# Output weight's sums on VectorE, three row groups prepared a quarter ahead, VectorE's order pinned in the output stage, results left in loaded operands

## The chip, the cores and the metric

The kernel runs on one core of a Trainium2 chip. A core has TensorE (PE, matrix products into PSUM banks), VectorE (DVE), ScalarE (ACT), GpSimd (POOL) and SyncE (SP), whose queue issues most of the DMAs. The metric is the device time of one execution in microseconds; lower is better.

## The reference

One layer of a decoder block on x of 2048 tokens by 1024 channels, in float32:

```python
mod = jax.nn.silu(c) @ w_ada + b_ada
shift, scale, gate = jnp.split(mod, 3, axis=-1)
h = rms_norm(x, norm_w) * (1.0 + scale) + shift
z = h @ w_in
a, b, g_conv, q, k, v, g_attn, m_conv, m_attn = jnp.split(z, SPLIT_POINTS, axis=-1)
u = depthwise_causal_conv(a * jax.nn.sigmoid(b), conv_w, conv_b)     # 31 taps
u = jax.nn.silu(layer_norm(u, conv_ln_w, conv_ln_b)) * jax.nn.silu(g_conv)
y_conv = u @ w_conv_out
# three groups of four heads, dilated causal windows, merged by their softmax denominators
o = ...
y_attn = (o * jax.nn.silu(g_attn)) @ w_attn_out
y = jax.nn.sigmoid(m_conv) * y_conv + jax.nn.sigmoid(m_attn) * y_attn
out = y @ w_out
x = x + gate * out
```

Only the last three products matter here: u @ w_conv_out, the merge into y, and y @ w_out with the gate and the residual.

## The kernel before

**Precision.** A float32 matrix product is made of three float32r products: each operand is split into a high part (ScalarE copies it into float32r, "h") and a low part (a subtraction, "l"), and h·h, h·l and l·h are added up in PSUM.

**The quarters.** The convolution branch is projected for four quarters of 512 tokens (`t` = 0 to 3), each in eight blocks `dm` of 128 output channels. A block is 24 matmuls of 512 columns (`project`, L1231) into a bank `yc`; six banks take turns. Behind a block VectorE multiplies the bank by the loaded gate `mc` (L1482), adds the loaded attention half `yl` (L1483), and SP stores the result to `y_d` (L1484). `yl` and the result `yc` both take their buffers from a ring of four named `yt`; `mc` has a ring of three.

**Normalising a quarter ahead.** While a quarter is projected, class `Norm` prepares the next: mean and squares on VectorE (`d`, `red`), a matmul `pc` of the squares, a copy `stf` on VectorE (L1269), two steps on GpSimd (L113, L114), a matmul `pr` that spreads the factor over the columns (L1276), and then per channel group `vf`, `tv` and the parts `u_kh`, `u_kl`. `d` is in the pool `lnp`, two buffers.

**The output stage.** y @ w_out is computed by a seven-product scheme on quarters of both matrices. For eight `j` (`out_quad`), token blocks j and j + 8 form four quarters of y, which are loaded as `yq`, combined on GpSimd (`ys`, L1422 to L1427) and split into `yh`, `yl` (`y_split`, L1431 and L1432). The weight's seven combinations are called B11, B21, T1, T2, T3, B22 and T4; each is held as `woh`/`wol` (or `wohi`/`wolo`) tiles for four row groups k. Products run in the order 0, 3, 2, 1, 4, 5, 6 on three banks: oa takes products 0, 2, 4 and 6, oc takes 3 and 5, ob takes 1. The sums of a bank go on growing from product to product, and between them VectorE adds the bank to a tile `xt`, which was loaded with the residual x (L1491); `xt` then goes to the output (L1496). So product 2, 4 and 6 each wait until VectorE has added what stood in oa.

**Preparing the weight.** `wo_fetch` loads 1 MB of `w_out` for a row group k (`wo_raw`), `wo_scale` multiplies it by the gate (L1375, two operations of 1024 columns), `wo_first` makes B11, B21 and T1 and computes T1 to T4 in place by four subtractions on GpSimd (L1400), and `wo_rest` splits T2, T3, B22 and T4 (L1390 and L1391). Row group 0 is loaded and scaled in the third quarter; groups 1 to 3 in the last. B22 and T4 can be split only when TensorE has read the last of the tiles whose place they take: in the last block, and at the end of it. The same holds for the parts of y with i from 2 on, which take the places of `u`. A hook `out_hooks(j)(i)` runs inside `product`: the part of y that is five products ahead, in the first quad also B22 (k = 1 and 3 on GpSimd) and T4, and the loads of the next quad.

**What sets the order.** TensorE's instructions stand in the order of the program. On the other engines a scheduler puts them into an order by its own estimate of when each is ready; an instruction passed to `keep_in_program_order` stays behind the one that the program has in front of it on its engine. Each engine then runs its list strictly in order. Pools hand out ring buffers; a DMA into a buffer waits until its last reader is done. `at_block(n, m, f)` calls f at matmul m of block n.

Of the kernel before, what the change touches and what calls it, by code (L numbers as in the profile page):

```python
# [10 lines left out]
F32 = mybir.dt.float32  # L11
F32R = mybir.dt.float32r
# [3 lines left out]
ALU = mybir.AluOpType  # L16
# [38 lines left out]
def tile_hybrid_block(  # L55
# [1244 lines left out]
    def at_block(n, m, f):  # L1300
        plan.setdefault(n, {}).setdefault(m, []).append(f)
# [63 lines left out]
            nc.sync.dma_start(last["gate"][c], gate_d[:, 512 * c : 512 * c + 512].to_broadcast([P, 512]))  # L1365

    def wo_fetch(k):
        w = sp.tile([P, S], F32, tag="wide", name="wo_raw0") if k == 0 else op.tile([P, S], F32, tag="raw", name=f"wo_raw{k}", bufs=4)
        w = wo_raw[k] = w.rearrange("p (h c n) -> p h c n", h=2, c=2)
        nc.sync.dma_start(w, w_out.rearrange("(h k p) (c n) -> k p h c n", h=2, p=P, c=2)[k])  # L1370

# [3 lines left out]
            nc.vector.tensor_tensor(w[:, :, c], w[:, :, c], last["gate"][c][:, None, :].to_broadcast([P, 2, 512]), op=ALU.mult)  # L1375

    def wo_place(name):
        if name in ("B11", "B21"):
            return [wop.tile([P, 4, 512], F32R, name=f"wo{hl}{name}") for hl in "hl"]
        if name == "T1":  # L1380
            return [op.tile([P, 4, 512], F32R, name=f"wo{hl}{name}", bufs=1) for hl in "hl"]
        if name == "T3":
            return [[wcp.tile([P, 512], F32R, tag=f"w{hl}{k}", name=f"wo{hl}{name}{k}") for k in range(4)] for hl in "hl"]
        return [quarter_tile(*{"T2": (0, 2), "B22": (0, 0), "T4": (1, 0)}[name], hl, f"wo{hl}{name}") for hl in ("hi", "lo")]

    def wo_split(name, k, src, eng=nc.vector):
        if name not in wo:
            wo[name] = wo_place(name)
        h, l = (x[k] if isinstance(x, list) else x[:, k] for x in wo[name])
        nc.scalar.activation(h, src, AF.Copy)  # L1390
        eng.tensor_tensor(l, src, h.bitcast(F32), op=ALU.subtract)  # L1391

    def wo_first(k):
        w = wo_raw[k]
        wo_split("B11", k, w[:, 0, 0])
        wo_split("B21", k, w[:, 1, 0])
        t1 = ys.tile([P, 512], F32, tag="fraw", name=f"wot1_{k}", bufs=3)
        for dst, x0, x1 in ((t1, w[:, 0, 1], w[:, 0, 0]), (w[:, 0, 0], w[:, 1, 1], w[:, 0, 1]), (w[:, 0, 1], w[:, 1, 1], t1),
                            (w[:, 1, 0], w[:, 1, 0], w[:, 0, 1])):
            nc.gpsimd.tensor_tensor(dst, x0, x1, op=ALU.subtract)  # L1400
        wo_split("T1", k, t1)

    def wo_rest(name, k, eng=nc.vector):
# [3 lines left out]
    LEAD = 5  # L1407

    def y_load(j):
        t = ysrc[j] = op.tile([P, S], F32, tag="raw", name=f"yq{j}", bufs=4).rearrange("p (q k t) -> p q k t", q=4, t=P)  # L1410
        for b in range(2):
            jj = j + NB // 2 * b
            nc.sync.dma_start(t[:, 2 * b : 2 * b + 2].rearrange("p q k t -> p (q k) t"),
                              y_d[:, :, P * jj : P * jj + P].rearrange("k p t -> p k t"))

    def y_split(j, i):
        a11, a12, a21, a22 = (ysrc[j][:, q].rearrange("p k t -> p (k t)") for q in range(4))
        pool_tt = nc.gpsimd.tensor_tensor
        n = WO_ORDER[i]
        if n == 0:  # L1420
            s1 = ysrc[j, "S1"] = ys.tile([P, 512], F32, tag="fraw", name=f"ys1_{j}", bufs=3)
            pool_tt(s1, a21, a22, op=ALU.add)  # L1422
            pool_tt(a21, a11, a21, op=ALU.subtract)
        if n == 2:
            pool_tt(a11, ysrc[j, "S1"], a11, op=ALU.subtract)
        if n == 4:
            pool_tt(a12, a12, a11, op=ALU.subtract)  # L1427
        src = (a11, a12, a11, ysrc[j, "S1"], a21, a12, a22)[n]
        own, tag, bufs = (op, "y", 2) if (j, i) in ((0, 0), (0, 1)) else (up[1], "u", KC)
        h, l = ya_of[j, n] = [own.tile([P, 512], F32R, tag=tag + hl, name=f"y{hl}{j}_{n}", bufs=bufs) for hl in "hl"]  # L1430
        nc.scalar.activation(h, src, AF.Copy)  # L1431
        nc.vector.tensor_tensor(l, src, h.bitcast(F32), op=ALU.subtract)  # L1432

    ysrc, ya_of, xin = {}, {}, {}

# [9 lines left out]
        xin[j, q] = t  # L1445

    at_block(12, 6, gate_rows)
    at_block(16, 6, lambda: wo_fetch(0))
    at_block(22, 6, lambda: wo_scale(0))

    for t in range(NT):
        tsl = slice(512 * t, 512 * t + 512)
        if t == NT - 1:
            lnp_c.__exit__(None, None, None)
            wop_c, wop = right("wop")
            ap_c.__exit__(None, None, None)
            up_c[1].__exit__(None, None, None)
            op_c = pool("op", bufs=2)
            op = op_c.__enter__()
            for k in range(1, 4):  # L1460
                at_block(KC * t, 2, lambda k=k: wo_fetch(k))
                at_block(KC * t + (1, 2, 3)[k - 1], 1, lambda k=k: wo_scale(k))
            for k in range(4):
                at_block(KC * t + (0, 1, 2, 4)[k], (3, 6, 15, 3)[k], lambda k=k: wo_first(k))
            for i, (name, k) in enumerate((b, k) for b in ("T2", "T3") for k in range(4)):
                at_block(KC * t + 4 + i // 2, 4 + 11 * (i % 2), lambda name=name, k=k: wo_rest(name, k))
            at_block(KC * t + 4, 8, lambda: y_load(0))
            for i in range(2):
                at_block(KC * t + 6, 6 + 6 * i, lambda i=i: y_split(0, i))
            for q in (0, 3):  # L1470
                at_block(KC * t + 5, 8, lambda q=q: x_load(0, q))
        for dm in range(KC):
            gt = gp.tile([P, 512], F32, tag="gt", name=f"mc{t}_{dm}")
            nc.sync.dma_start(gt, mc_d[dm, :, tsl])
            ya = ys.tile([P, 512], F32, tag="yt", name=f"yl{t}_{dm}", bufs=4)
            nc.sync.dma_start(ya, ya_d[dm, :, tsl])
            pz = bank("zso"[dm % 3], f"yc{t}_{dm}")
            sl = slice(P * (dm % 4), P * (dm % 4) + P)
            project(pz, [h[:, sl] for h, _ in wc[dm // 4]], [l[:, sl] for _, l in wc[dm // 4]],
                    norms[t].uh, norms[t].ul, plan.get(KC * t + dm))  # L1480
            yt = ys.tile([P, 512], F32, tag="yt", name=f"yc{t}_{dm}", bufs=4)
            nc.vector.scalar_tensor_tensor(yt, gt, 1.0, pz, op0=ALU.add, op1=ALU.mult)  # L1482
            nc.vector.tensor_add(yt, yt, ya)  # L1483
            nc.sync.dma_start(y_d[dm, :, tsl], yt)  # L1484

    HB = NB // 2

    def out_quad(j, hooks):
        pa, pb, pc = bank("z", f"oa{j}"), bank("s", f"ob{j}"), bank("o", f"oc{j}")
        x11, x12, x21, x22 = (xin.pop((j, q)) for q in range(4))  # L1490
        add = lambda dst, ps: nc.vector.tensor_tensor(dst, dst, ps, op=ALU.add)  # L1491
        begun = set()

        def store(q, t):
            jj, c = j + HB * (q // 2), q % 2
            nc.sync.dma_start(out2[P * jj : P * jj + P, 512 * c : 512 * c + 512], t)  # L1496

        def product(n, ps, more=False):
            yh, yl = ya_of.pop((j, n))
            wh, wl = ([x[k] if isinstance(x, list) else x[:, k] for k in range(4)] for x in wo[PRODUCTS[n][1]])  # L1500
            yh, yl = ([y[:, P * k : P * k + P] for k in range(4)] for y in (yh, yl))
            terms = [t for k in range(4) for t in ((yh[k], wh[k]), (yh[k], wl[k]), (yl[k], wh[k]))]
            for m, (y, w) in enumerate(terms):
                nc.tensor.matmul(ps, y, w, start=(m == 0 and ps.name not in begun), stop=(m == 11 and not more),  # L1504
                                 skip_group_check=True)
            begun.add(ps.name)
            hooks(WO_ORDER.index(n))

        product(0, pa, True)
        add(x11, pa)  # L1510
        product(3, pc, True)
        add(x22, pc)
        product(2, pa, True)
        add(x12, pa)
        product(1, pb)
        add(x11, pb)
        store(0, x11)
        product(4, pa, True)
        add(x22, pa)
        store(3, x22)  # L1520
        product(5, pc)
        add(x12, pc)
        store(1, x12)
        product(6, pa)
        add(x21, pa)
        store(2, x21)

    for q in (1, 2):
        x_load(0, q)
# [3 lines left out]
    def out_hooks(j):  # L1533
        def f(i):
            if j == 0 and i < 2:
                for k in (2 * i, 2 * i + 1):
                    wo_rest("B22", k, (nc.vector, nc.gpsimd)[k % 2])
            elif j == 0 and i < 6:
                wo_rest("T4", i - 2)
            if j + 1 < HB and i == 0:  # L1540
# [15 lines left out]
    wop_c.__exit__(None, None, None)  # L1556
    wcp_c.__exit__(None, None, None)
    hpool_c[0].__exit__(None, None, None)

# [27 lines left out]
```

## Time and profile before

| | |
|---|---|
| time, median of 3 runs | 2428.23 us (2424.98 to 2432.36) |
| profiled execution | 2423.63 us, span 2421.7 us |
| PE / DVE / ACT / POOL busy | 2372.0 / 1734.9 / 998.0 / 839.7 us |
| mean granted TensorE clock | 0.994 |
| last quarter of the projection | about 2205 to 2250 us |
| output stage | about 2250 us to the end |

Times in a timeline are microseconds from the start of the span: start, length, engine, line, operation, written tile <- read tiles, and in brackets how long the engine had been idle and what ended that. Tiles appear there without their numbers, so `yl` is both the loaded attention half and a low part of y; the line tells which.

### The profile page before, as it was taken

To read this page: it belongs to the slowest core of one execution; us is meant where nothing else is said; L and a number is where in the kernel's file an instruction comes from. 1 tells how busy PE (TensorE), PEld (TensorE's weight loads), DVE (VectorE), ACT (ScalarE), POOL (GpSimd) and SP (SyncE) were. 2 spreads that over 40 slices of the span, in tenths; PEclk is the share of its full clock that TensorE was granted. 3 is DMA by queue.
4 is the path that set the end of the run, shared out by engine and by line. 5 is a ranking of instruction groups with operands and counts; after the bars stand their busy time and mean duration, and the time that the engine had idled before them with its cause. 6 is when DMAs were issued, how large, how long until landed. Compare 5 with 4: busy or idle time off the path is not lost. (4 is left out here: it accounts for less than half of the span.)

```text
span 2421.7 us, 39474 instructions
## 1 busy us (share of the span) xinstructions
PE 2372.0 (98%) x12785; PEld 2117.9 (87%) x12785; DVE 1734.9 (72%) x3941; ACT 998.0 (41%) x2790; POOL 839.7 (35%) x949
## 2 busy tenths in 40 slices
PE   6999999999999999999999999999999999999899
PEld 2989999999999999999888888878888888888687
DVE  5865655555555565567779999989999977787643
ACT  4833433343343444344544444554444444431221
POOL 3421111111111111112467777775565620004420
PEclk8999999999999999999999999999999999999999
DMA  7633543454453222115664544674444469865742
GB/s 256 219 115 110 158 128 102 142 150 140 145 154 89 70 67 61 31 49 176 211 207 138 164 154 133 211 231 125 136 150 132 156 221 315 285 198 185 215 145 83
DMA packets 349468, 372.99 MB, mean 154 GB/s; under 512 B 29704, under 2 KB 251176, under 8 KB 349262
## 3 DMA queue, kind: packets, MB, share of 16 engines
q1 hardware_dynamic: 335966, 346.80, 46.1%
q10 hardware_dynamic: 13296, 23.66, 2.7%
q8 instruction: 102, 1.67, 0.3%
q14 instruction: 104, 0.85, 0.1%
HBM read 231.74 MB, written 138.61 MB: 153 GB/s over the span
## 5 line engine op out<-in xcount | busy, mean ns | idle before, releaser
L370 PE MATMUL pz<-wh_u,hT_lo 128*128 128x384 f32 x1536 | 537.1, 350 | 5.2 <-DVE hT_lo L289 3.8
L370 PE MATMUL pz<-wh_u,hT_hi 128*128 128x384 f32 x1536 | 518.3, 337 | 5.3 <-ACT wh_u L346 2.9
L370 PE MATMUL pz<-wl_u,hT_hi 128*128 128x384 f32 x1536 | 518.9, 338 | 0.6 <-DVE wl_u L349 0.6
L398 DVE SCALAR_TENSOR_TENSOR qk<-pz,st,wqk 128x128 f32<-128x128 f32 x384 | 117.0, 346 | 318.3 <-POOL st L114 318.1
L113 POOL TENSOR_SCALAR st<-st 128x2 f32<-128x2 f32 x192 | 47.3, 247 | 812.7 <-ACT sq L387 812.7
L370 PEld LDWEIGHTS pz<-wh_u,hT_hi 128*128 128x128 f32 x1536 | 290.7, 189 | 8.2 <-ACT wh_u L346 3.6
L370 PEld LDWEIGHTS pz<-wh_u,hT_lo 128*128 128x128 f32 x1536 | 289.4, 188 | 8.1 <-DVE hT_lo L289 4.6
L370 PEld LDWEIGHTS pz<-wl_u,hT_hi 128*128 128x128 f32 x1536 | 289.8, 189 | 2.0 <-DVE wl_u L349 1.5
L434 ACT ACTIVATE qkT<-ptq 128x256 f32<-128x256 f32 x192 | 73.6, 383 | 420.2 <-PE ptq L432 419.7
L1033 DVE SCALAR_TENSOR_TENSOR ce<-us,pair_taps,ce 128x512 f32<-128x512 f32 x240 | 179.8, 749 | 1.7
L1004 DVE SCALAR_TENSOR_TENSOR ce<-ut,chan,ce 128x512 f32<-128x512 f32 x240 | 179.5, 748 | 0.0
L1017 DVE SCALAR_TENSOR_TENSOR cq<-ut,chan,cq 128x512 f32<-128x512 f32 x208 | 156.5, 752 | 4.2
L919 POOL TENSOR_TENSOR slT<-wT,shT 128x512 fp32r<-128x512 f32 x97 | 129.4, 1336 | 75.3 <-ACT shT L918 75.3
L387 ACT ACTIVATE sq<-pz 128x128 bf16<-128x128 f32 x384 | 106.0, 276 | 99.6 <-PE pz L370 92.6
L114 POOL TENSOR_TENSOR st<-st,mhalf 128x2 f32<-128x2 f32 x192 | 136.6, 712 | 16.0
L918 ACT ACTIVATE shB<-wB 128x512 fp32r<-128x512 f32 x120 | 75.5, 631 | 152.0 <-issue 44.5
L918 ACT ACTIVATE shT<-wT 128x512 fp32r<-128x512 f32 x100 | 63.1, 631 | 153.0 <-issue 66.2
L919 POOL TENSOR_TENSOR slB<-wB,shB 128x512 fp32r<-128x512 f32 x77 | 102.4, 1330 | 68.5 <-ACT shB L918 67.1
L447 ACT ACTIVATE sm<-sm,osb 128x128 f32<-128x128 f32 (+1 forms) x192 | 88.7, 462 | 62.6 <-DVE osb L445 59.6
L461 PE MATMUL po<-lv,pT 128*128 128x128 f32 x600 | 97.2, 273 | 0.0
L461 PEld LDWEIGHTS po<-lv,pT 128*128 128x128 f32 x600 | 93.0, 189 | 0.5 <-issue 0.5
L445 DVE CUSTOM_DVE_ANT_0 sm<-ps,mask 128x128 f32<-128x128 f32 (+1 forms) x192 | 68.7, 358 | 26.5 <-PE ps L442 26.4
(666 smaller groups left out, 6331.5 us busy)
## 6 DMA issues: line engine op xcount, KB each, us to landing
wB<-in_w_in_dram SPq DMA_DIRECT2D x140, 256.0 KB, 3.3
qkv_d<-qkv SPq DMA_DIRECT2D x128, 192.0 KB, 2.2
wT<-tT_d SPq DMA_DIRECT2D x80, 256.0 KB, 2.7
raw_u<-in_w_in_dram SPq DMA_DIRECT2D x93, 192.0 KB, 2.8
lqk<-qkv_d SPq DMA_DIRECT2D x128, 128.0 KB, 2.3
tT_d<-wB ACTq DMA_DIRECT2D x60, 256.0 KB, 2.8
acc_d<-osb SPq DMA_DIRECT2D x192, 65.0 KB, 1.8
at<-acc_d SPq DMA_DIRECT2D x64, 195.0 KB, 3.5
```

The lines of the kernel that those rows point to most:

```text
L114: nc.gpsimd.tensor_tensor(dst, scratch[:, :n], mhalf[:, :n], op=ALU.pow)
L370: nc.tensor.matmul(pz[:, :width], part(a, k, P * j, P), w[:, :width], start=(m == 0), stop=(m == 23))
L387: nc.scalar.activation(sq, pz[:, P * i : P * i + P], AF.Square, scale=1.0 / math.sqrt(P), accum_out=st[:, i : i + 1])
L398: nc.vector.scalar_tensor_tensor(qk[:, 2 * i : 2 * i + 2].rearrange("p a b -> p (a b)"), pz[:, P * i : P * i + P], st[:, 2 + i : 3 + i], w ...
L434: nc.scalar.activation(qkT.rearrange("p a b -> p (a b)"), pt[:, :256], AF.Copy)
L447: nc.scalar.activation(sm[:, :w], sm[:, :w], AF.Exp, scale=-1.0, bias=o[:, P : P + 1], accum_out=o[:, P + 1 : P + 2])
L461: nc.tensor.matmul(po[:, :P], box["pT"][:, P * i : P * i + P], vt, start=(i == 0), stop=(i == nk - 1))
L918: nc.scalar.activation(h, q[name], AF.Copy)
L919: eng.tensor_tensor(l, q[name], h.bitcast(F32), op=ALU.subtract)
L1004: stt(box["e"], e[:, 1 + j : 513 + j], chan[:, cb, 2 * j : 2 * j + 1], box["e"], op0=ALU.mult, op1=ALU.add)
L1017: stt(box["o"], o[:, 2 + j : 514 + j], w, psum_o, op0=ALU.mult, op1=ALU.add)
L1033: stt(dst, box["both"][:, 1 + j : 513 + j], pair_taps[:, cb, j : j + 1], box["e"], op0=ALU.mult, op1=ALU.subtract if j == 0 else ALU.add)
```

## The change

1. The four subtractions of `wo_first` run on VectorE, and so do all low parts of B22. GpSimd has nothing of the weight left.
2. Row groups 1 and 2 are loaded into one buffer of `lnp` (`d`, which `Norm` of the third quarter has left) and scaled in the third quarter of the program's text, as group 0 is. Only group 3 is loaded in the last quarter. B11 takes the other buffer of `lnp`, and B21 moves into the pool `op`. The ring `raw` of `op` has two buffers where it had four: after group 3 it holds `yq` alone.
3. A block's product is written into the loaded `mc` tile and the result into the loaded `yl` tile, which is then stored. The ring `yt` holds loads only.
4. In `out_quad` the hook runs behind the add that follows a product, where it ran in front of it. The adds, the low parts of T4 and those of y from the first quad's sixth on are kept in program order.

```diff
     def wo_fetch(k):
-        w = sp.tile([P, S], F32, tag="wide", name="wo_raw0") if k == 0 else op.tile([P, S], F32, tag="raw", name=f"wo_raw{k}", bufs=4)
+        if k == 0:
+            w = sp.tile([P, S], F32, tag="wide", name="wo_raw0")
+        elif k < 3:
+            if k == 1:
+                last["d"] = lnp.tile([P, 2, S], F32, tag="d", name="wo_raw12", bufs=2)
+            w = last["d"][:, k - 1]
+        else:
+            w = op.tile([P, S], F32, tag="raw", name=f"wo_raw{k}")
...
     def wo_place(name):
-        if name in ("B11", "B21"):
-            return [wop.tile([P, 4, 512], F32R, name=f"wo{hl}{name}") for hl in "hl"]
-        if name == "T1":
+        if name == "B11":
+            both = lnp.tile([P, 2, 4, 512], F32R, tag="d", name="woB11", bufs=2)
+            return [both[:, i] for i in range(2)]
+        if name in ("B21", "T1"):
             return [op.tile([P, 4, 512], F32R, name=f"wo{hl}{name}", bufs=1) for hl in "hl"]
...
-        eng.tensor_tensor(l, src, h.bitcast(F32), op=ALU.subtract)
+        ins = eng.tensor_tensor(l, src, h.bitcast(F32), op=ALU.subtract)
+        if name == "T4" and eng is nc.vector:
+            tc.keep_in_program_order(ins)
...
-            nc.gpsimd.tensor_tensor(dst, x0, x1, op=ALU.subtract)
+            nc.vector.tensor_tensor(dst, x0, x1, op=ALU.subtract)
...
-        t = ysrc[j] = op.tile([P, S], F32, tag="raw", name=f"yq{j}", bufs=4).rearrange("p (q k t) -> p q k t", q=4, t=P)
+        t = ysrc[j] = op.tile([P, S], F32, tag="raw", name=f"yq{j}").rearrange("p (q k t) -> p q k t", q=4, t=P)
...
-        nc.vector.tensor_tensor(l, src, h.bitcast(F32), op=ALU.subtract)
+        ins = nc.vector.tensor_tensor(l, src, h.bitcast(F32), op=ALU.subtract)
+        if (j, i) >= (0, LEAD):
+            tc.keep_in_program_order(ins)
...
-    at_block(16, 6, lambda: wo_fetch(0))
-    at_block(22, 6, lambda: wo_scale(0))
+    for k in range(3):
+        at_block(16 + k, 9, lambda k=k: wo_fetch(k))
+        at_block((18, 20, 22)[k], 6, lambda k=k: wo_scale(k))
...
-            for k in range(1, 4):
-                at_block(KC * t, 2, lambda k=k: wo_fetch(k))
-                at_block(KC * t + (1, 2, 3)[k - 1], 1, lambda k=k: wo_scale(k))
+            at_block(KC * t, 2, lambda: wo_fetch(3))
+            at_block(KC * t + 2, 1, lambda: wo_scale(3))
...
-            yt = ys.tile([P, 512], F32, tag="yt", name=f"yc{t}_{dm}", bufs=4)
-            nc.vector.scalar_tensor_tensor(yt, gt, 1.0, pz, op0=ALU.add, op1=ALU.mult)
-            nc.vector.tensor_add(yt, yt, ya)
-            nc.sync.dma_start(y_d[dm, :, tsl], yt)
+            nc.vector.scalar_tensor_tensor(gt, gt, 1.0, pz, op0=ALU.add, op1=ALU.mult)
+            nc.vector.tensor_add(ya, ya, gt)
+            nc.sync.dma_start(y_d[dm, :, tsl], ya)
...
-        add = lambda dst, ps: nc.vector.tensor_tensor(dst, dst, ps, op=ALU.add)
+        add = lambda dst, ps: tc.keep_in_program_order(nc.vector.tensor_tensor(dst, dst, ps, op=ALU.add))
...
-            hooks(WO_ORDER.index(n))
 
         product(0, pa, True)
         add(x11, pa)
+        hooks(0)
         product(3, pc, True)
         add(x22, pc)
+        hooks(1)
...
-                    wo_rest("B22", k, (nc.vector, nc.gpsimd)[k % 2])
+                    wo_rest("B22", k)
```

The scheduler's new order is seen at three places. The first is VectorE at the start of the output stage. Names there carry their numbers: `yl0_5` is the low part of product 5's operand in quad 0, `xt0_0` the residual tile of quad 0's first quarter, `oa0` the bank. Before:

```order
L1391 TENSOR_TENSOR woloB22_25502<-wo_raw2_25107,wohiB22_25501 128x512
L1482 SCALAR_TENSOR_TENSOR yc3_7_25464<-mc3_7_25431,yc3_7_25435 128x512
L1432 TENSOR_TENSOR yl0_5_25511<-yq0_25309,yh0_5_25510 128x512
L1432 TENSOR_TENSOR yl0_6_25532<-yq0_25309,yh0_6_25531 128x512
L1483 TENSOR_TENSOR yc3_7_25464<-yc3_7_25464,yl3_7_25433 128x512
L1391 TENSOR_TENSOR woloT4_25549<-wo_raw0_24744,wohiT4_25548 128x512
L1391 TENSOR_TENSOR woloT4_25549<-wo_raw1_25105,wohiT4_25548 128x512
L1391 TENSOR_TENSOR woloT4_25549<-wo_raw2_25107,wohiT4_25548 128x512
L1491 TENSOR_TENSOR xt0_0_25349<-xt0_0_25349,oa0_25486 128x512
L1391 TENSOR_TENSOR woloT4_25549<-wo_raw3_25109,wohiT4_25548 128x512
L1491 TENSOR_TENSOR xt0_3_25351<-xt0_3_25351,oc0_25488 128x512
```

The same place after:

```order
L1399 TENSOR_TENSOR woloB22_25465<-wo_raw3_25084,wohiB22_25464 128x512
L1491 SCALAR_TENSOR_TENSOR mc3_7_25394<-mc3_7_25394,yc3_7_25398 128x512
L1442 TENSOR_TENSOR yl0_5_25474<-yq0_25275,yh0_5_25473 128x512
L1442 TENSOR_TENSOR yl0_6_25495<-yq0_25275,yh0_6_25494 128x512
L1492 TENSOR_TENSOR yl3_7_25396<-yl3_7_25396,mc3_7_25394 128x512
L1500 TENSOR_TENSOR xt0_0_25314<-xt0_0_25314,oa0_25448 128x512
L1500 TENSOR_TENSOR xt0_3_25316<-xt0_3_25316,oc0_25450 128x512
L1500 TENSOR_TENSOR xt0_1_25430<-xt0_1_25430,oa0_25448 128x512
L1399 TENSOR_TENSOR woloT4_25512<-wo_raw0_24731,wohiT4_25511 128x512
L1442 TENSOR_TENSOR yl1_0_25519<-yq1_25470,yh1_0_25518 128x512
L1500 TENSOR_TENSOR xt0_0_25314<-xt0_0_25314,ob0_25449 128x512
L1399 TENSOR_TENSOR woloT4_25512<-wo_raw12_24776,wohiT4_25511 128x512
```

The low parts of T4 have moved from in front of the first add to behind the third, and each later one stands between two adds, in turn with a part of the next quad's y; B22 and the two last parts of this quad's y stay in front of the first add. In front of the upper rows, B22 has four low parts on VectorE where it had two.

The second place is VectorE in the second quarter, around the copy `stf3` with which the last quarter's variance leaves PSUM. Before:

```order
L1261 TENSOR_TENSOR red3_24391<-red3_24391,sq3_7_24419 128x512
L1482 SCALAR_TENSOR_TENSOR yc1_5_24625<-mc1_5_24585,yc1_5_24589 128x512
L1483 TENSOR_TENSOR yc1_5_24625<-yc1_5_24625,yl1_5_24587 128x512
L1269 COPY stf3_24651<-pc3_24646 128x4
L1482 SCALAR_TENSOR_TENSOR yc1_6_24678<-mc1_6_24629,yc1_6_24633 128x512
```

The same place after, `wo_raw12` being row groups 1 and 2 and `wot1_1` the t1 of group 1:

```order
L1261 TENSOR_TENSOR red3_24382<-red3_24382,sq3_7_24410 128x512
L1382 TENSOR_TENSOR wo_raw12_24776<-wo_raw12_24776,gate0_24536 128x2x512
L1382 TENSOR_TENSOR wo_raw12_24776<-wo_raw12_24776,gate1_24537 128x2x512
L1491 SCALAR_TENSOR_TENSOR mc1_5_24572<-mc1_5_24572,yc1_5_24576 128x512
L1410 TENSOR_TENSOR wot1_1_25142<-wo_raw12_24776 128x512
L1269 COPY stf3_24637<-pc3_24632 128x4
L1492 TENSOR_TENSOR yl1_5_24574<-yl1_5_24574,mc1_5_24572 128x512
```

A scaled pair and a subtraction now stand in front of the copy; the pair of group 2 stands behind it.

The third place is SP's queue at the start of the output stage. Before:

```order
L1444 DMA xt0_2_25470<-in_x_dram 128x512
L1413 DMA yq1_25507<-y_d_81 128x8x128 x2
L1484 DMA y_d_81<-yc3_7_25464 128x512
L1444 DMA xt1_0_25574<-in_x_dram 128x512
L1444 DMA xt1_1_25576<-in_x_dram 128x512
L1413 DMA yq2_25663<-y_d_81 128x8x128 x2
```

The same place after:

```order
L1423 DMA yq1_25470<-y_d_81 128x8x128
L1493 DMA y_d_81<-yl3_7_25396 128x512
L1423 DMA yq1_25470<-y_d_81 128x8x128
L1456 DMA xt1_1_25540<-in_x_dram 128x512
L1456 DMA xt1_2_25542<-in_x_dram 128x512
L1456 DMA xt1_3_25544<-in_x_dram 128x512
L1456 DMA xt2_1_25686<-in_x_dram 128x512
L1505 DMA out_0_dram<-xt0_0_25314 128x512
L1505 DMA out_0_dram<-xt0_3_25316 128x512
L1505 DMA out_0_dram<-xt0_1_25430 128x512
L1423 DMA yq2_25626<-y_d_81 128x8x128 x2
```

The load of `yq2` has moved behind three stores of the first quad, and the two halves of `yq1` have the last block's store between them.

More of the change, by code (lines that the diff above doesn't have):

```diff
@@ L1453, in tile_hybrid_block @@
         if t == NT - 1:
-            lnp_c.__exit__(None, None, None)
-            wop_c, wop = right("wop")
             ap_c.__exit__(None, None, None)
@@ L1506, in product @@
             begun.add(ps.name)
-            hooks(WO_ORDER.index(n))
         product(0, pa, True)
         add(x11, pa)
+        hooks(0)
         product(3, pc, True)
         add(x22, pc)
+        hooks(1)
         product(2, pa, True)
         add(x12, pa)
+        hooks(2)
         product(1, pb)
@@ L1517, in out_quad @@
         store(0, x11)
+        hooks(3)
         product(4, pa, True)
@@ L1520, in out_quad @@
         store(3, x22)
+        hooks(4)
         product(5, pc)
@@ L1523, in out_quad @@
         store(1, x12)
+        hooks(5)
         product(6, pa)
@@ L1526, in out_quad @@
         store(2, x21)
+        hooks(6)
     for q in (1, 2):
@@ L1555, in tile_hybrid_block @@
     ys_c.__exit__(None, None, None)
-    wop_c.__exit__(None, None, None)
+    lnp_c.__exit__(None, None, None)
     wcp_c.__exit__(None, None, None)
```

## The prediction

> **What bounds the kernel now.** I read the page's busy table first, then PE's waits after 2000 us, and then the stretch around the one that is there, engine by engine.
>
> ```profile
> PE 2372.0 (98%) x12785; PEld 2117.9 (87%) x12785; DVE 1734.9 (72%) x3941; ACT 998.0 (41%) x2790; POOL 839.7 (35%) x949
> ...
> PE oa L1504 <- DVE xt L1491: 8.9, 1, 8.9
> ```
>
> The first row is the page's; the second is the only row that the waits of PE give for everything after 2000 us. TensorE is busy for 98% of the span, so an edit to other engines is worth only what TensorE now waits for them, and in the part of the program that the diff touches this is one wait. The timeline of PE and the chain show it and what follows it:
>
> ```profile
> 2255.22 0.39 PE L1504 MATMUL oc<-wohT,yl 128*128 128x512 f32 x1
> 2264.53 0.77 PE L1504 MATMUL oa<-wohiT,yh 128*128 128x512 f32 x1 [8.92 <-DVE xt L1491]
> ...
> 2264.53 5.21 PE oa L1504 x12
> 2269.74 2.81 PE ob L1504 x12
> ...
> 2240.00:2260.00 20.00, 15.61 (x67) 12.26 (x66) 16.08 (x22) 7.07 (x13) 5.92 (x4) 0.98 0.56 172
> 2260.00:2280.00 20.00, 15.46 (x57) 12.39 (x58) 14.85 (x20) 4.30 (x8) 8.25 (x7) 0.77 0.96 272
> 2280.00:2300.00 20.00, 20.00 (x88) 16.10 (x87) 10.85 (x15) 4.43 (x7) 11.65 (x8) 1.00 0.67 202
> ```
>
> (In the last three: window, length, then busy time of PE, PEld, DVE, ACT, POOL, the granted clock, DMA share, GB/s.) The output stage's first quad has run product 0 into bank oa and product 3 into oc. Product 2 writes oa again, so it waits for VectorE's add xt0_0, which reads oa: 8.92 us. The 12 matmuls behind the wait take 5.21 us, the next 12 take 2.81, and the granted clock of that window is 0.77. So the wait costs twice: 8.92 + (5.21 - 2.81 = 2.40) = 11.3 us.
>
> Why the add was late is in VectorE's own timeline, with one row of POOL and two of ACT:
>
> ```profile
> 2233.21 6.87 DVE L1391 TENSOR_TENSOR wolT<-wo_raw,wohT 128x512 fp32r<-128x512 f32 x4
> 2242.30 2.48 DVE L1391 TENSOR_TENSOR woloT<-wo_raw,wohiT 128x512 fp32r<-128x512 f32 x4
> 2247.40 0.69 DVE L1482 SCALAR_TENSOR_TENSOR yc<-mc,yc 128x512 f32<-128x512 f32 x1
> 2250.90 0.69 DVE L1483 TENSOR_TENSOR yc<-yc,yl 128x512 f32<-128x512 f32 x1 [2.82 <-DMA yl<-ya_d]
> 2252.54 0.69 DVE L1482 SCALAR_TENSOR_TENSOR yc<-mc,yc 128x512 f32<-128x512 f32 x1 [0.94 <-DMA y_d<-yc]
> 2253.87 1.89 DVE L1432 TENSOR_TENSOR yl<-yq,yh 128x512 fp32r<-128x512 f32 x3
> 2255.68 3.43 DVE L1391 TENSOR_TENSOR woloB<-wo_raw,wohiB 128x512 fp32r<-128x512 f32 x2
> 2259.62 1.76 DVE L1432 TENSOR_TENSOR yl<-yq,yh 128x512 fp32r<-128x512 f32 x2
> 2261.91 1.88 DVE L1391 TENSOR_TENSOR woloT<-wo_raw,wohiT 128x512 fp32r<-128x512 f32 x3
> 2263.72 0.67 DVE L1491 TENSOR_TENSOR xt<-xt,oa 128x512 f32<-128x512 f32 x1
> ...
> 2255.30 1.58 POOL L1427 TENSOR_TENSOR yq<-yq 128x512 f32<-128x512 f32 x1 [14.07 <-DVE yl L1432]
> ...
> 2245.24 1.98 ACT L1431 ACTIVATE yh<-yq 128x512 fp32r<-128x512 f32 x3 [10.15 <-PE yc L1231]
> 2247.13 2.18 ACT L1390 ACTIVATE wohiB<-wo_raw 128x512 fp32r<-128x512 f32 x4
> ```
>
> Product 0 ended at about 2252.7 (2255.45 less one product of 2.80), the add ran at 2263.72. Three causes stand in the rows. VectorE stood still for 2.82 and 0.94 us, for a load into and a store out of the four buffers that loads and results share. Four subtractions take 6.87 us where POOL works beside them and 2.48 where it does not (1.72 against 0.62 each). And three low parts of T4, needed only by product 6, stood in front of the add. ACT's rows show what cannot come sooner: it had the y halves by 2247.2, when TensorE had let go of their slots, and those of B22 by 2249.3.
>
> **The change, part by part.** *Sums from GpSimd to VectorE.* By group, POOL's rows of the last quarter (the first t1 lies earlier):
>
> ```profile
> L1400 POOL TENSOR_TENSOR wo_raw<-wo_raw 128x512 f32<-128x512 f32 x8 | 13.8, 1723 | 28.8 <-DVE wolB L1391 28.7
> L1400 POOL TENSOR_TENSOR wo_raw<-wo_raw,wot 128x512 f32<-128x512 f32 x4 | 6.7, 1687 | 0.2
> L1400 POOL TENSOR_TENSOR wot<-wo_raw 128x512 f32<-128x512 f32 x3 | 4.6, 1546 | 29.8 <-DVE wo_raw L1375 29.8
> ```
>
> 25.1 us leave POOL there, and the two B22 parts besides. VectorE gets 16 sums and 2 low parts, 18 x 0.62 = 11.2 us, and loses the 1.1 us that each operation beside POOL paid. From 2205 to 2245.8 the new order gives it 41 operations of 512 columns and two of 1024: 41 x 0.62 + 2.4 = 27.8 us of 40.6. It fits, so TensorE pays nothing.
>
> *Rows loaded and scaled a quarter ahead.* Two scaled pairs and two t1 sums move into the second quarter, where one pair and a sum stand in front of the copy that starts the last quarter's variance:
>
> ```profile
> 2129.17 2.36 DVE L1375 TENSOR_TENSOR wo_raw<-wo_raw,gate 128x1024 f32<-128x1024 f32 x2
> 2138.63 0.74 DVE L1286 SCALAR_TENSOR_TENSOR vf<-d,chan,rs 128x512 f32<-128x512 f32 x1
> 2145.64 0.68 DVE L1261 TENSOR_TENSOR red<-red,sq 128x512 f32<-128x512 f32 x1
> 2150.78 0.16 DVE L1269 COPY stf<-pc 128x4 f32<-128x4 f32 x1 [2.25 <-PE pc L1267]
> ...
> 2151.34 1.02 POOL L114 TENSOR_TENSOR stf<-stf,mhalf 128x4 f32<-128x4 f32 x1
> ...
> 2156.24 1.05 PE L1276 MATMUL pr<-ident,stf 128*128 128x128 f32 x8
> ...
> wo_raw<-in_w_out_dram SPq DMA_DIRECT2D x4, 1024.0 KB, 4.8
> yq<-y_d SPq DMA_DIRECT2D x16, 512.0 KB, 5.7
> out_dram<-xt SPq DMA_DIRECT2D x32, 256.0 KB, 3.5
> ```
>
> The slot of row groups 1 and 2 is read last at 2138.63, so I estimate the fetch at 2140.6 and its landing at 2145.4, 4.8 later. The pair then runs behind the last red add, 2146.3 to 2148.7, and the copy keeps its time. At worst the pair waits for both fetches, 2140.6 + 2 x 4.8 = 2150.2; pair, one multiply and the sum take 3.7, the copy and POOL's two steps 1.6: 2155.5, still before TensorE's pr at 2156.24. So 0 to about 0; a gain is excluded, since TensorE does not wait there now. SP holds gg, mc and y_d transfers behind the fetch for about 1 us; their users come a block of 24 matmuls (5.6 us) later.
>
> *Results over loaded operands.* The four yt buffers now hold loads only and the result leaves from them, so a load can be three blocks ahead; the 2.82 and 0.94 us go. mc buffers are held one operation (0.69) longer, which a period of 5.6 us hides.
>
> *The pin, and two yq buffers.* In the new order of VectorE ten operations stand between yl3_6 and xt0_0. From the ACT rows: three y parts end at 2247.9, four B22 parts at 2250.3, or 2251.4 with POOL's L1427 beside one of them; then mc3_7, yl0_5, yl0_6 and yl3_7 (4 x 0.62) and the add: 2254.5. Product 2 can start at 2255.45. The wait is gone with 1.0 us to spare. The T4 parts now stand between the adds of the quad. The fourth follows the add behind product 5, at about 2266.7 + 0.1 + 0.67 + 0.68 = 2268.2; product 6 reaches its tenth matmul at 2269.0. Next late is yq1: SP can issue its second half at about 2254.9, it lands at 2260.6 (5.7), and POOL's and VectorE's times are in these rows:
>
> ```profile
> 2267.62 1.27 POOL L1422 TENSOR_TENSOR ys<-yq 128x512 f32<-128x512 f32 x1 [7.39 <-DMA yq<-y_d]
> ...
> 2270.39 1.80 DVE L1432 TENSOR_TENSOR yl<-ys,yh 128x512 fp32r<-128x512 f32 x1
> ...
> 2295.68 0.34 SPq L1496 DMA_DIRECT2D out_dram<-xt  x1
> 2298.86 0.33 SPq L1444 DMA_DIRECT2D xt<-in_x_dram  x1
> ```
>
> 2260.6 + 1.3 + 0.6 (ACT) + 1.8 = 2264.3, and the pinned add of product 4 behind it ends at 2265.0, before product 6 at 2266.65: 1.6 us to spare.
>
> The sum is 11.3 us: 2423.63 of the profiled execution becomes 2412.3. The median of the runs shown lies 4.6 us above that execution, so on that footing it is 2416.9; I say 2417.
>
> [...] The trace shows 2.40, and I use that.
>
> **The rivals.** *A: part of the wait stays.* The pin does not put xt0_0 in front: B22 and the y parts still precede it, with 1.0 us of slack. If all seven operations with two SBUF operands ran at 1.72, the add would end at 2247.9 + 7 x 1.72 + 1.35 = 2261.3, TensorE would wait 5.8 us, and 5.8 + 2.4 of the 11.3 would stay: a gain of 3.1, 2425.1. Against it: POOL has one operation left in that stretch. I take 0.17, at 2418 to 2425. [...]
>
> *B: SP becomes the bound of the output stage, slower.* With two yq buffers each yq load now queues behind the quad's four x loads, and each of those waits for an output store out of its slot: 2295.68 to 2298.86 is one link, 3.2 us, with 3.5 the median landing. Four links are 14 us of a quad's 7 x 2.80 = 19.6. The rival decides where a link passes 4.9 us. At 6 us a quad takes 24 plus the yq issue; VectorE's pinned order passes the lateness on to TensorE, 4.4 us in each of six quads, 26.4 - 11.3 = 15 us slower: 2443. For it: DMA share 0.96 early in the stage. Against it: links of 3.2 in this trace, share 0.67 in the next window of the table. 0.10.
>
> *C: it gives back as much in the second quarter*, if the row fetch lands 15 us late and pr waits for it: about 2428, 0.05.
>
> **How the numbers follow.** The forecast has 0.68. 0.3% (7.3 us) is about what a measurement of this kernel can tell from no change; the three runs shown spread by that much. Faster by more: nearly all of the forecast (0.66) and 0.04 of A: 0.70. Within: the rest of A, C and 0.01 of the forecast: 0.20. Slower: 0.10 from B. The range: 2411 is the profiled sum of 2412.3 less about one; 2427 takes in A and leaves out B and most of C.
>
> **What would show it.** Right: no wait of PE for xt in the first quad, its third product 2.8 us long, clock 1.00 in every window from 2240 on, no L1400 rows of POOL, VectorE without waits for yl or y_d in the last quarter. Wrong: a wait of PE for xt or for woloT between 2245 and 2275, a wait for pr near 2156, or one in each quad with SP's yq issue late.

## The result, and the profile after

The changed kernel takes 2416.06 us (median of 6 runs, 2414.91 to 2420.42) against 2427.14 of the kernel before: a ratio of 0.9954 [0.9942, 0.9967]. Timed again later on one chip it took 2416.13 (5 runs) against 2426.22, 0.9958 [0.9945, 0.9970]. The forecast was 2417. Its profiled execution took 2415.89, span 2414.0.

The busy row of its page, and then all that PE waits for after 2000 us (line, releaser; us in total, times, longest):

```profile
PE 2374.5 (98%) x12785; PEld 2119.2 (88%) x12785; DVE 1727.6 (72%) x3959; ACT 995.1 (41%) x2790; POOL 809.4 (34%) x931
...
PE pr L1276 <- POOL stf L114: 0.8, 1, 0.8
PE pc L1267 <- DVE red L1261: 0.3, 1, 0.3
```

The wait for xt, 8.92 us before, is gone; two small waits have come, both in front of the last quarter. The first quad on PE's timeline and in the chain, and the two windows:

```profile
2253.79 0.62 PE L1513 MATMUL oa<-woB,yh 128*128 128x512 f32 x2
2256.59 0.40 PE L1513 MATMUL oc<-wohT,yh 128*128 128x512 f32 x1
2259.35 0.40 PE L1513 MATMUL oa<-wohiT,yh 128*128 128x512 f32 x1
2262.16 0.40 PE L1513 MATMUL ob<-wohB,yh 128*128 128x512 f32 x1
...
2259.51 2.81 PE oa L1513 x12
...
2240.00:2260.00 20.00, 20.00 (x87) 16.14 (x86) 11.75 (x17) 7.11 (x13) 1.71 (x1) 1.00 0.41 128
2260.00:2280.00 20.00, 20.00 (x87) 16.14 (x87) 12.91 (x19) 5.04 (x9) 7.39 (x6) 1.00 0.73 228
```

Products 0, 3 and 2 follow each other without a gap; PE is busy for all 20 us of both windows, and the granted clock is 1.00 where it was 0.98 and 0.77. VectorE's rows that answer to those of before, and the one operation that POOL has left in that stretch:

```profile
2249.80 2.03 DVE L1442 TENSOR_TENSOR yl<-yq,yh 128x512 fp32r<-128x512 f32 x3
2251.75 3.59 DVE L1399 TENSOR_TENSOR woloB<-wo_raw,wohiB 128x512 fp32r<-128x512 f32 x4
2255.27 0.67 DVE L1491 SCALAR_TENSOR_TENSOR mc<-mc,yc 128x512 f32<-128x512 f32 x1
2255.87 1.28 DVE L1442 TENSOR_TENSOR yl<-yq,yh 128x512 fp32r<-128x512 f32 x2
2257.08 0.68 DVE L1492 TENSOR_TENSOR yl<-yl,mc 128x512 f32<-128x512 f32 x1
2257.68 0.67 DVE L1500 TENSOR_TENSOR xt<-xt,oa 128x512 f32<-128x512 f32 x1
...
2251.28 1.71 POOL L1437 TENSOR_TENSOR yq<-yq 128x512 f32<-128x512 f32 x1 [23.72 <-DVE yl L1442]
```

The add of xt0_0 ends at 2258.35, 1.0 us before product 2. The rest of the account stands where the last quarter is made ready. From the chain (DMA), from SP's timeline (SPq), from VectorE's and from PE's:

```profile
2127.06 8.90 DMA wo_raw<-in_w_out_dram
2150.53 8.39 DMA wo_raw<-in_w_out_dram
...
2132.71 6.58 SPq L1284 DMA_DIRECT2D gg<-g_d  x2
2148.41 0.38 SPq L1377 DMA_DIRECT2D wo_raw<-in_w_out_dram  x1
...
2135.98 2.36 DVE L1382 TENSOR_TENSOR wo_raw<-wo_raw,gate 128x1024 f32<-128x1024 f32 x2 [2.10 <-DMA wo_raw<-in_w_out_dram]
2138.26 0.68 DVE L1290 SCALAR_TENSOR_TENSOR vf<-tv,gg 128x512 f32<-128x512 f32 x1
2154.55 2.36 DVE L1382 TENSOR_TENSOR wo_raw<-wo_raw,gate 128x1024 f32<-128x1024 f32 x2 [2.27 <-DMA wo_raw<-in_w_out_dram]
2158.03 0.15 DVE L1269 COPY stf<-pc 128x4 f32<-128x4 f32 x1
...
2160.03 1.16 PE L1276 MATMUL pr<-ident,stf 128*128 128x128 f32 x8 [0.84 <-POOL stf L114]
```

Row group 0's fetch lands late and VectorE waits 2.10 us for it. Behind that scaling stands the vf that frees a gg buffer, so SP holds a load of gg for 6.58 us, and all that is queued behind: row group 1 is fetched at 2148.41. VectorE waits again, 2.27, and the copy stf runs at 2158.03; pr is 0.84 late.

Why row group 0 is fetched late stands in the chain and in SP's own waits. First what SP's loads of `yl` wait for between 2105 and 2160, before and after (us in total, times, longest), then two rows of the chain after:

```profile
SPq L1476 <- DMA y_d<-yc: 2.5, 1, 2.5
...
SPq L1486 <- DMA y_d<-yl: 23.4, 9, 3.9
...
2114.61 3.84 DMA y_d<-yl
2118.95 4.44 DMA gg<-g_d
```

The result now leaves from the buffer of the loaded `yl`, so the next load into that buffer waits for the store out of it, and SP's queue stands still meanwhile. Between the third pr and the fetch of row group 0 there are four such waits, 10.4 us in all, where there was none before. The chain leads to the fetch from one of them: the store of 3.84 us, then the load of gg that stood behind it, then VectorE's work on it. The fetch comes 16.2 us behind the third pr, where it came 13.2 us behind it.

Stretch by stretch, from the starts of the same matmuls in PE's timelines (the four pr are those of the four quarters; before, they start at 2009.18, 2056.79, 2108.62 and 2156.24):

| us | before | after | difference |
|---|---|---|---|
| up to the first pr, untouched by the change | 2009.18 | 2011.40 | +2.2 |
| first to third pr | 99.44 | 99.47 | 0.0 |
| third to fourth pr | 47.62 | 49.16 | +1.5 |
| fourth pr to product 0 | 93.66 | 93.76 | +0.1 |
| products 0, 3 and 2 | 19.68 | 8.37 | -11.3 |
| rest | 152.12 | 151.84 | -0.3 |
| span | 2421.7 | 2414.0 | -7.7 |

### The profile page after: what moved, and what is told of

It is laid out like the page before. It is cut to its first block, busy times and chain, and to the rows that moved or that the text cites. A ratio compares the mean times of both kernels' runs of the same rounds, so it can differ in the third digit from the quotient of the medians.

```text
span 2414.0 us, 39453 instructions
## 1 busy us (share of the span) xinstructions
PE 2374.5 (98%) x12785; PEld 2119.2 (88%) x12785; DVE 1727.6 (72%) x3959; ACT 995.1 (41%) x2790; POOL 809.4 (34%) x931
## 4 chain that ended last, share of the span: by engine, by line
PE 90%; DMA 5%; DVE 2%; ACT 2%; POOL 1%; issue 1%; SPq 0%; ACTq 0%; DVEq 0%; POOLq 0%
PE pz L370 31%; PE paab L955 7%; PE yc L1231 6%; PE oa L1513 4%; PE ya L1231 4%; PE pag_g_d L955 4%; PE pag_mc_d L955 4%; PE pcab L955 3%; PE pag_ma_d L955 3%; PE pzg L370 3%; PE ps L442 3%; PE po L461 3%; PE oc L1513 2%; PE pcg_mc_d L955 2%; PE pcg_g_d L955 2%; PE ptq L432 2%
```

## The experiments

Two times without any wait serve as the measure: 47.6 us from the third pr to the fourth, and 8.37 us for products 0, 3 and 2; both are called undisturbed. Theory T: the wait for xt0_0 was a sum of delays on VectorE (POOL beside it, the shared ring, T4 in front of the add), and that wait with its cold clock (0.77 granted from 2260 to 2280 in the kernel before) is the whole price. Rivals: R1, POOL beside VectorE alone; R2, the order alone; R3, the ring alone; R4, the loading ahead. The upstream part ("to pr 1") varies by 5.7 us between runs, so runs of one execution are compared by stretches; "wait" is PE's wait for xt at product 2. All but before, after and f1 are single executions; the kernel before, run beside them, took 2427.07 (d1, d3, d4 and u4), 2426.82 (u1, u2, u3 and f1, median of 8) and 2423.15 (s6 and s16).

| kernel | us | to pr 1 | pr 3 to pr 4 | products 0, 3, 2 | wait | rest |
|---|---|---|---|---|---|---|
| before | 2423.63 | 2009.2 | 47.62 | 19.68 | 8.92 | 152.1 |
| after | 2415.89 | 2011.4 | 49.16 | 8.37 | 0 | 151.8 |
| d1_sums | 2421.30 | 2012.9 | 47.61 | 9.88 | 1.30 | 155.8 |
| d3_results | 2435.03 | 2014.6 | 52.77 | 20.00 | 9.26 | 152.7 |
| d4_pin | 2427.74 | 2013.5 | 47.61 | 19.31 | 9.16 | 152.1 |
| u4_no_pin | 2417.29 | 2011.5 | 48.76 | 9.39 | 0.81 | 151.9 |
| u1_sums_back | 2424.94 | 2014.5 | 55.35 | 8.36 | 0 | 151.9 |
| u2_no_ahead | 2422.15 | 2013.2 | 48.97 | 12.78 | 2.67 | 152.1 |
| u3_results_back | 2414.26 | 2010.4 | 47.61 | 8.37 | 0 | 151.9 |
| f1_scale_kept | 2412.68 | 2008.9 | 47.62 | 8.36 | 0 | 152.1 |
| s6_delay | 2418.39 | 2010.5 | 47.61 | 13.48 | 3.34 | 151.8 |
| s16_delay | 2426.93 | 2009.1 | 47.61 | 23.33 | 12.60 | 151.8 |

**One part alone, on the kernel before.** d1_sums:

```diff
-            nc.gpsimd.tensor_tensor(dst, x0, x1, op=ALU.subtract)
+            nc.vector.tensor_tensor(dst, x0, x1, op=ALU.subtract)
-                    wo_rest("B22", k, (nc.vector, nc.gpsimd)[k % 2])
+                    wo_rest("B22", k)
```

> The kernel before with the sums and B22 on VectorE and nothing else. Theory T (the wait for the add xt0_0 is a sum of delays on VectorE: POOL beside it, the shared load ring, T4 in front of the add): the slow-down beside POOL goes, VectorE is no longer behind, the three T4 parts and some of the ring stay, so TensorE waits 2 to 5 us for xt instead of 8.9. Rival R1 (POOL beside VectorE is the whole cause): no wait. Rival R2 (only the order of T4 and the add matters): 8 to 9 us as before.

Two rows of its PE timeline, the first matmul of product 2 and of product 6:

```profile
2260.68 0.47 PE L1504 MATMUL oa<-wohiT,yh 128*128 128x512 f32 x1 [1.30 <-DVE xt L1491]
...
2274.02 0.48 PE L1504 MATMUL oa<-wohiT,yh 128*128 128x512 f32 x1 [1.90 <-DVE xt L1491]
```

The sums alone take the wait from 8.92 to 1.30, but a new one of 1.90 comes at product 6 and the rest grows by 3.6 us. R1 explains most of the wait, not all; T, with 2 to 5 us at product 2, had put the sums too low.

d3_results, the result left in the loaded operands:

```diff
-            yt = ys.tile([P, 512], F32, tag="yt", name=f"yc{t}_{dm}", bufs=4)
-            nc.vector.scalar_tensor_tensor(yt, gt, 1.0, pz, op0=ALU.add, op1=ALU.mult)
-            nc.vector.tensor_add(yt, yt, ya)
-            nc.sync.dma_start(y_d[dm, :, tsl], yt)
+            nc.vector.scalar_tensor_tensor(gt, gt, 1.0, pz, op0=ALU.add, op1=ALU.mult)
+            nc.vector.tensor_add(ya, ya, gt)
+            nc.sync.dma_start(y_d[dm, :, tsl], ya)
```

> The kernel before with results left in the loaded operands and nothing else. Theory T: the idle 2.8 and 0.9 us of VectorE go, the rest stays: TensorE waits about 5 us (4 to 6) for xt. R1 and R2: 8 to 9 us, as before. Rival R3 (the ring is the whole cause): under 1 us.

The wait stays, 9.26 us, so R3 falls, and so do the 4 to 6 us of T. VectorE no longer waits for `yl` or for a store near the end, but one wait of 1.42 us has come in their place, at the last block but one (first row below). The row names PE, but that block's matmuls had ended at 2254.9. What came late is its `mc`: the operation that frees the buffer stood 3.0 us behind the product of an earlier block (2255.13 and 2258.13), and the load was issued at 2259.21.

And pr 3 to pr 4 grows by 5.2 us, with only row group 0 loaded there as before: 1.81 of it is PE's wait for pc, the rest the slow restart behind it, in which matmuls of 512 columns start 0.43 us apart instead of 0.23. The other VectorE and SP rows show the same pair as those of after, the scaling that waits and the held gg:

```profile
2263.48 0.69 DVE L1481 SCALAR_TENSOR_TENSOR mc<-mc,yc 128x512 f32<-128x512 f32 x1 [1.42 <-PE oa L1503]
...
2140.18 2.36 DVE L1375 TENSOR_TENSOR wo_raw<-wo_raw,gate 128x1024 f32<-128x1024 f32 x2 [1.97 <-DMA wo_raw<-in_w_out_dram]
...
2131.44 0.44 SPq L1370 DMA_DIRECT2D wo_raw<-in_w_out_dram  x1
2137.04 6.45 SPq L1284 DMA_DIRECT2D gg<-g_d  x2
```

d4_pin, the hooks behind the adds and the order kept (that of the T4 and y parts too, as in the change):

```diff
-        add = lambda dst, ps: nc.vector.tensor_tensor(dst, dst, ps, op=ALU.add)
+        add = lambda dst, ps: tc.keep_in_program_order(nc.vector.tensor_tensor(dst, dst, ps, op=ALU.add))
         product(0, pa, True)
         add(x11, pa)
+        hooks(0)
...
```

> The kernel before with the hooks behind the adds and VectorE's order kept, and nothing else. Theory T: the three T4 parts (1.9 us) leave from in front of the add, TensorE waits about 7 us (6 to 8) for xt. R2: no wait. R1 and R3: 8 to 9 us.

It waits 9.16 us: alone the pin brings nothing, and R2 falls. T's 6 to 8 us are missed too.

**One part undone, on the kernel after.** u4_no_pin (d4's edit reversed):

> The changed kernel with the hooks in front of the adds again and no order kept. Theory T: three T4 parts (1.9 us) come in front of an add that had 1.0 us to spare, so TensorE waits about 0.9 us (0 to 2) for xt and its clock stays at 1.00. R2: a wait near 8.9 us comes back. R1 or R3: none at all.

0.81 us of wait come back, 1.0 with what follows, as T had it: this is what the pin is worth once VectorE is otherwise early.

u1_sums_back (d1's edit reversed):

> The changed kernel with the sums and two B22 parts back on POOL. Theory T: three row groups are scaled early, so most sums of POOL lie where VectorE has time; near the end only B22 is beside it, and the add is late by 0 to 2 us. R1 (POOL beside VectorE is what matters): over 3 us of wait for xt.

No wait for xt: with the rows prepared ahead, even sums on POOL are over in time. So R1 alone is not needed either. What comes instead lies at the fourth pr, 7.7 us more than undisturbed, of which 4.8 are PE's wait for pc and the rest the slow restart; PE's wait and, on VectorE, its cause:

```profile
PE pc L1267 <- DVE red L1261: 4.8, 1, 4.8
...
2156.88 2.36 DVE L1382 TENSOR_TENSOR wo_raw<-wo_raw,gate 128x1024 f32<-128x1024 f32 x2 [1.97 <-DMA wo_raw<-in_w_out_dram]
2159.16 0.69 DVE L1261 TENSOR_TENSOR red<-red,sq 128x512 f32<-128x512 f32 x1
```

Here the scaling of a late row group stands in front of the last red, where in the changed kernel it stands behind it, so pc is late as well.

u2_no_ahead (the kernel before with the edits of d1, d3 and d4, that is, the change without its second point):

> The changed kernel with row groups 1 to 3 loaded and scaled in the last quarter again, as before; sums on VectorE, results in loaded operands and the kept order stay. Theory T: VectorE has room for it, no wait for xt; and in the second quarter the waits for pc and pr (0.3 and 0.8 us) are gone, since no fetch stands in front of the variance. Rival R4 (loading ahead is what freed the add): over 3 us of wait for xt.

2.67 us of wait remain, 4.4 with what follows. Of that, 1.46 is a wait for a gate:

```profile
2254.02 0.69 DVE L1485 SCALAR_TENSOR_TENSOR mc<-mc,yc 128x512 f32<-128x512 f32 x1 [1.46 <-DMA mc<-mc_d]
```

So loading ahead is a part of the gain, 4.4 us here. Neither text had it so: T expected no wait, R4 over 3 us. T also expected no wait for pc once the fetches were gone; there is one of 1.12 us, and the stretch is 48.97.

u3_results_back (d3's edit reversed):

> The changed kernel with the result of a block in a buffer of its own from the four yt again. Theory T: VectorE is not behind, so stores out of the ring are done in time; wait for xt 0 to 1.5 us. R3 (the ring is the whole cause): 2.8 us or more.

No wait for xt, and none near the fourth pr: the stretch is 47.61. SP has the two next row groups out at 2140.9, as I had estimated for the change itself, with all of the loading ahead still in:

```profile
2123.76 0.38 SPq L1377 DMA_DIRECT2D wo_raw<-in_w_out_dram  x1
2140.89 0.90 SPq L1377 DMA_DIRECT2D wo_raw<-in_w_out_dram  x2
```

Together with d3 this puts the loss on the third point, the results over loaded operands. Row group 0's fetch comes 13.2 us behind the third pr in before, d1, d4 and u3. With results over operands it comes 13.7 (s6), 14.2 (s16), 15.2 (u4), 15.8 (f1), 15.9 (u1), 16.2 (after), 17.0 (u2) and 17.4 us (d3) behind it. Up to 14.2 the stretch is undisturbed, though gg is held there as well (6.42 us in s6); from 15.2 on time is lost in all but f1, whose scalings stand elsewhere. So in these executions the edit delays every fetch, and it costs time only where the delay is large.

**More delay, to price a wait.** In front of the first add of quad 0, N subtractions more (6 and 16), which repeat one low part of T2:

```diff
         product(0, pa, True)
+        if j == 0:
+            h, l = (x[:, 3] for x in wo["T2"])
+            for _ in range(N):
+                tc.keep_in_program_order(nc.vector.tensor_tensor(l, wo_raw[3][:, 0, 1], h.bitcast(F32), op=ALU.subtract))
         add(x11, pa)
```

> The changed kernel with six extra subtractions (a low part of T2 written again with the same values) around the first add of quad 0, so that the add comes late by about 2.7 us. Theory T (a wait costs its length, and a cold clock on top only if it is long): TensorE waits about 2.7 us for xt, the 12 matmuls behind it take 2.8 to 3.0 us, the clock stays at 1.00. Rival (any wait costs a warm-up): 12 matmuls in about 5 us.

> The same with sixteen extra subtractions, so that the add comes late by about 8.7 us. Theory T: TensorE waits about 8.7 us, the 12 matmuls behind the wait take about 5.2 us, granted clock near 0.77 in that window of 20 us; the span is about 11 us longer than that of the changed kernel, so the whole gain is lost. Rival (the price of the wait was something else, such as stores or loads late behind it): the span grows by under 8 or over 14 us.

All of them stand in front of the add, four among the parts of B22 and y; the add of oc (xt0_3) has moved in front of it too. So the add is later than the texts say: the waits are 3.34 and 12.60, not 2.7 and 8.7. The add of oc, 0.7 us, is what s6 has more; the other 3.2 us of s16 are not shown. The three products take 5.11 and 14.96 more than undisturbed: 1.77 and 2.36 above the wait itself. Everything behind stays the same (151.8), so one wait here costs its length and a slow restart, nothing later; that part of T is shown. That a short wait leaves the clock alone is not: behind 3.34 us the 12 matmuls took 4.43 us, where T had 2.8 to 3.0, and the granted clock was 0.91 from 2260 to 2280. Behind 12.60 they took 5.02.

The slow restart by the length of the wait, at the waits for xt: 0.2 at 0.81 and at 1.30; 1.8 at 1.90 (d1's product 6); 1.7 at 2.67; 1.8 at 3.34 and at 9.16; 2.4 at 8.92, 9.26 and 12.60. At the waits for pc near the fourth pr: 0.2 at 1.12 (u2), 3.4 at 1.81 (d3), 2.9 at 4.81 (u1).

**The scalings later.** f1_scale_kept, on the kernel after, keeps the three scalings in program order; they then start at 2173.8 to 2196.9, in the third quarter, behind the fourth pr:

```diff
-            nc.vector.tensor_tensor(w[:, :, c], w[:, :, c], last["gate"][c][:, None, :].to_broadcast([P, 2, 512]), op=ALU.mult)
+            ins = nc.vector.tensor_tensor(w[:, :, c], w[:, :, c], last["gate"][c][:, None, :].to_broadcast([P, 2, 512]), op=ALU.mult)
+            if k < 3:
+                tc.keep_in_program_order(ins)
```

> The changed kernel with the scaling of row groups 0, 1 and 2 kept at its place in the program (third quarter), where the scheduler had moved it into the second. Theory T: the variance no longer stands behind a fetch; TensorE's waits for pc and pr in the second quarter go (1.1 us), VectorE has room in the third quarter, nothing else changes: about 1.5 us faster than the changed kernel, 0.995 of before or a little less. Rival: the sums then come so late in the last quarter that xt0_0 is late again, a wait for xt of over 1 us.

2412.68 us (5 runs, 2410.80 to 2416.09), 0.9943 [0.9929, 0.9957] against the kernel before; there is no wait for xt, so the rival of the text falls. On SP the hold of gg shrinks and both row groups go out eight to ten microseconds earlier, counted from the third pr; the stretch is 47.62:

```profile
2130.64 2.12 SPq L1284 DMA_DIRECT2D gg<-g_d  x2
2138.63 1.04 SPq L1377 DMA_DIRECT2D wo_raw<-in_w_out_dram  x2
```

So the link between late fetch and late copy is the scaling's place on VectorE: taken out, the results may stay in the operands.

**The changed kernel against f1 and u3 together.** L: the late rows cost time; J: the lower times were chance. ("Product 3" in the two texts should read product 1, the fourth to run.)

> The changed kernel itself, timed beside the next one on the same chip. By the reading of the runs so far its second quarter can lose time: where the scaling of a late row group stands ahead of the copy stf on VectorE, the stretch from the third pr to the fourth is 49.2 us (after), 48.8 (without the pin), 47.6 (both kernels with added subtractions); undisturbed it is 47.6. So theory L (late rows on VectorE's queue) expects this stretch between 47.6 and 49.2 us here, no wait for xt at product 2, 8.37 us from product 0 to product 3, and a median 1 to 3 us above the next kernel's. The rival J (the loss in that stretch is chance, and the lower times of the two variants were where the runs before it happened to start) expects medians within 1 us of each other.

> The changed kernel with the first three row groups' scalings kept in program order (they then run in the third quarter) and the results back in their own yt tiles. Theory L expects no wait for pr or pc near 2150 and a stretch of 47.6 us from the third pr to the fourth in every profile, no SyncE hold of a gg load beyond 3 us between 2130 and 2140, no wait for xt at product 2 (results in yt tiles left none in the kernel that put only them back), 8.37 us from product 0 to product 3, and a median 1 to 3 us below the changed kernel's. The rival J expects it within 1 us of the changed kernel's. A theory that the results over loaded operands are needed for the xt wait expects a wait of 1 us or more at product 2 here.

a0_after, the changed kernel: 2416.13 (2414.98 to 2418.34). g1_kept_own: 2414.19 (2412.50 to 2415.43), 0.9945 [0.9932, 0.9959] against the kernel before, and below the changed kernel in 23 of the 25 pairs. The median's 1.9 us are what L says. The two profiled executions do not carry it: the stretch is 47.81 and 47.61, and 0.2 us is all that differs there. In a0 VectorE is as held as ever:

```profile
2132.77 6.49 SPq L1284 DMA_DIRECT2D gg<-g_d  x2
...
2154.79 2.36 DVE L1382 TENSOR_TENSOR wo_raw<-wo_raw,gate 128x1024 f32<-128x1024 f32 x2 [2.52 <-DMA wo_raw<-in_w_out_dram]
2158.27 0.15 DVE L1269 COPY stf<-pc 128x4 f32<-128x4 f32 x1
```

but there PE came to this place 1.6 us later than in after (third pr at 2112.46 against 2110.87), so that the copy at 2158.27 was nearly in time. By these two runs the late rows set the time of pr, and PE pays only when it is early. s6 and s16, with an earlier fetch and no loss, fit that. What the average price is, between 0 and 1.9 us, stays open. g1 has no wait for xt either, so the results over loaded operands are not needed against it. Both variants beat the kernel before; over the changed kernel their lead is of the size of the scatter.

## Why the prediction was right, and where not

**The main term** was 8.92 + 2.40 = 11.3; the first quad lost 19.68 - 8.37 = 11.3. The medians fell by 11.1. The profiled executions fell by 7.7 only, because this one of after started 2.2 late upstream and lost 1.5 in front of the fourth pr. The wait and its cold restart thus went as forecast, term by term. That the median came within 1 us of the forecast is in part luck: the sum leaves out the loss in front of the fourth pr (1.5 us in this execution, 0.2 in a0), and timed again on one chip the medians fell by 10.1.

**VectorE's times.** Product 0 starts 3.89 later than before. Shifted by that, the add was forecast to end at 2258.4 and ended at 2258.35; the fourth T4 part at 2272.1, measured 2271.44 + 0.68 = 2272.12, and PE waits for none; the y part behind yq1 at 2268.2, measured 2268.37. One of the four B22 parts ran beside POOL's L1437 and the four took 3.59 us: three of 0.68 and one of 1.79, which began 0.5 us into POOL's 1.71 us. It took 1.1 us longer than the others, the 1.1 us that the rows of before had for one part beside POOL.

**The step that failed** is the one on results over loaded operands, in three ways. It credited the edit with 2.82 and 0.94 us of VectorE's idle time as part of the gain; d3 and u3 show that the wait for xt does not depend on it. It took the loads to run three blocks ahead, since the ring holds loads only. But the loads now wait for the stores out of their buffers: nine of them, 23.4 us of SP's time, between 2105 and 2160. So the fetch of row group 0 slid 3 us, the scaling, which stood in front of vf before as well, now had to wait for it, and gg was held 6.6 us. And it named only mc as held longer, by one operation, which the block's period would hide. The waits of 1.46 us in u2 and 1.42 in d3 show that the period did not hide that either.

**Loading ahead at 0** holds by itself (u3: 47.61), but not beside the third point. I had the next fetch at 2140.6, or 2142.9 with the later start of this run's stretch, and a landing of 4.8, at worst 9.6 for both; they were issued at 2148.41 and 2150.53, and the second took 8.39. My bound 2155.5 for the worst case left that hold out. A wait for pr near 2156 was named as a sign of being wrong, and it came, with 0.84 us. Rival C so came true in small: 1.5 us of the 11 that it would have given back.

**The other rivals.** A: without the pin 0.81 us of the wait stays (u4), so the 1.0 us of slack was rightly seen as thin. B: SP's links from output store to x load in the second quad reach 3.6 us, below 4.9, and PE waits nowhere in the output stage:

```profile
2291.55 0.42 SPq L1505 DMA_DIRECT2D out_dram<-xt  x1
2295.11 0.33 SPq L1456 DMA_DIRECT2D xt<-in_x_dram  x1
```

The chances that the prediction gives for "within" add up to 0.13 + 0.05 + 0.01 = 0.19, not 0.20.

**The theory behind it.** T stands in one form only: no single cause made the wait. Its delays do not add up part by part: the expectations of d1, d3, d4 and u2, which took them so, were all missed. The sums alone take 7.6 of 8.9 us; without them, the other three points take all of it; the loading ahead is worth 2.67, and the pin 0.81, when the rest is in. What u1 lost by giving the sums back lies elsewhere, at the fourth pr.

## What to carry to other kernels

A wait that several delays cause is best priced by undoing each part from the finished version, not by doing each alone: the pin was worth nothing alone and 1 us at the end. Where an edit changes which buffer a result leaves from, follow the DMA queue in its order and the scheduler's new list behind it: here one operation that waited 2.10 us for a late transfer, in front of one that frees a buffer, had the queue held for 6.58 us, and the next transfer was later still (issued at 2148.41, 2140.89 in u3). And compare single executions stretch by stretch: the untouched first 2009 us alone differed by up to 5.7 us between runs.

## What the runs showed of the hardware that was not expected

The slow restart does not grow evenly with the wait's length. Behind the waits of 0.81 to 1.30 us above it is 0.2 us; behind those of 1.81 to 12.60 it lies between 1.7 and 3.4, and 12.60 costs less (2.4) than 1.81 did in d3 (3.4). In u2, after a wait of 2.67, the first matmuls were still at full speed, 0.31 and 0.23 us from start to start; those of 2264.77 to 2267.33 had 0.43 us each, and from 2268.07 on it was 0.23 again. The granted clock there was 0.76, 0.50, 0.50 and 0.53 in the four microseconds from 2264 on, and 1.00 on either side. In the kernel before the slow matmuls lasted 4.8 us (2264.53 to 2269.35). Waits of 1.90 us in d1 and of 1.81 in d3, there followed by the eight one-column matmuls of pc, were enough for a slow restart (1.8 and 3.4 us). What sets the size stays open.

A 1 MB row group landed in 4.8 us at the median before; the three of the changed kernel near the third and fourth pr took 8.9, 6.1 and 8.4 us.
